# Half of the input ahead of the first weights, the SSM's swaps of halves in SyncE's queue, and the last LayerNorm pass in halves on VectorE

## The chip, the cores and the metric

The kernel runs on one core of one Trainium2 chip. The metric is the time of one execution in device microseconds, the median of three runs. The profile is that of one further execution, recorded by the hardware profiler.

## What is computed

Two decoder layers over x of 256 tokens by 1024 channels, all in float32. In each layer a mixer and a feed-forward part stand one behind the other, and each is modulated by shift, scale and gate columns that are computed from the conditioning vector c. Inside the mixer a state-space model (SSM, a diagonal complex scan) and a sparse attention run side by side on one input projection. Cut to what matters:

```python
cond_in = jax.nn.silu(c)
for l in range(DEPTH):
    mod = cond_in @ w_cond[l] + b_cond[l]              # 6 x 1024 columns
    sh1, sc1, gt1, sh2, sc2, gt2 = split(mod, 6)
    u = x * (1.0 + sc1) + sh1
    z = u @ w_in[l]                                    # u_ssm, q, k, v, index q/k/w, two gates
    y_ssm = s5_branch(u_ssm, ...)                      # scan over time, GELU, GLU
    y_attn = dsa_branch(q, k, v, q_idx, k_idx, w_idx)  # top-64 keys of each query, attention
    h = (sigmoid(g_ssm) * (y_ssm @ p_ssm) + sigmoid(g_attn) * (y_attn @ p_attn)) @ w_out[l]
    x = layer_norm(ALPHA * x + (1 + gt1) * h, ln1_g[l], ln1_b[l])
    u = x * (1.0 + sc2) + sh2
    f = (silu(a) * b) @ w_down[l]                      # a, b = split(u @ w_gate_up[l])
    x = layer_norm(ALPHA * x + (1 + gt2) * f, ln2_g[l], ln2_b[l])
return x
```

## The kernel before, in words

The tokens are held as two tiles of 128 rows: `X[:, 0]` and `X[:, 1]`, each 128 x 1024. Every product with a weight is done in three passes with a high and a low part of both operands (`hi`, `lo`, `aTh`, `aTl`). A weight block of 512 KB is loaded into a `raw` tile by a DMA that SyncE issues (L351), ScalarE casts it to `hi` (L388), VectorE subtracts to get `lo` (L389), and TensorE multiplies (L1396, L1476). The blocks stand in one list; a pump (`st.pump_dma`) issues the next loads of that list, as many as there are free tiles, so what stands first in the program stands first in SyncE's queue. SyncE works its queue in order, and a load whose tile is not free yet holds up those behind it.

**The start.** c is loaded, then the conditioning's weights (`w_cond`, 512 KB a block) and the first blocks of `w_in`. TensorE transposes X in 16 pieces (L1527: four of the first half, then twelve that need the second half too), transposes constants of the SSM (L546, L567), and makes the first columns of the modulation from four `w_cond` blocks, which the program calls group 0 here (L448, 32 matmuls); then come the first products of the input projection (L1547), and group 1 of the modulation from the next four blocks (L448 again). The first half of x is loaded in ScalarE's queue (L1566), the second in SyncE's (L1568).

**The SSM's scan** (`ssm_run`). For each of two halves h = 0, 1 there is a set of tiles 128 x 512, which the traces call `s` (h = 0) and `k` (h = 1). Per half VectorE multiplies by cosine and sine (L863, L864), adds (L865) and scans along time (L866). Then `swap_halves` copies the scan's result with partitions 0 to 63 and 64 to 127 exchanged into another tile of the set, by two DMAs of 128 KB (L508, L509). Later VectorE multiplies the scan's result by the cosine (`s2`, L872), the swapped tile by the sine (`s3`, L873), and subtracts (`s4`, L878); TensorE reads what `s4` wrote (L886). `swap_halves` is also called twice while the SSM of layer 1 is prepared, around 330 us. Where `s2`, `s3` and `s4` stand in VectorE's order among the other work (the `lo` subtractions, the indexer's scores `sco` L1044, the rounds of top-k L1049 and L1050) is decided by the program's own order of steps when it is built.

**The end.** `ln_out(t)` is the last LayerNorm for each of the two token tiles: mean and variance (L1247, L1248), a power -0.5 on GpSimd (L1249), then columns 0 to 831 in two passes on VectorE and columns 832 to 1023 by ScalarE and GpSimd, with one store each from SyncE.

Of the kernel before, what the change touches and what calls it, by code (L numbers as in the profile page):

```python
# [10 lines left out]
AF = mybir.ActivationFunctionType  # L11
ALU = mybir.AluOpType
# [3 lines left out]
D = 1024  # L16
# [156 lines left out]
def kernel(  # L173
# [11 lines left out]
    V, A, P, PE, SP = nc.vector, nc.scalar, nc.gpsimd, nc.tensor, nc.sync  # L185
    NRAW, NHL, AHEAD = 6, 4, 2
    LO_P = (1, 2)
    OUT_A = 832
    GLU_AT = "ga0"
    DENSE = ((None, 2, 2, 2, 2, 2, 2, 2, 2, 2, 2), (2, 4, 4, 4, 4, 2), (2, 4, 4, 4, 4, 4, 4, None, None, None, None),  # L190
             (None,) * 6)
# [19 lines left out]
    def sbt(shape, tag, dt=F32, bufs=1):  # L211
        return sb.tile(shape, dt, tag=tag, bufs=bufs, name=nm(tag))
# [79 lines left out]
    def start(gen):  # L292
        t = Task(gen)
        tasks.append(t)
        return t
# [100 lines left out]
    st = Stream()  # L396
# [108 lines left out]

    def swap_halves(o, i):

        P.dma_start(o[0:64], i[64:128])  # L508
        P.dma_start(o[64:128], i[0:64])  # L509


    ssm = [dict() for _ in range(depth)]
# [1 line left out]
    def ssm_prep(l, w0, w, we):  # L514
# [72 lines left out]
        if l == 0:  # L587
            V.tensor_scalar(X1, pc, sg1, None, ALU.mult)
            A.copy(X2, turned_c(1))
        else:  # L590
            A.copy(cc, pc)
            V.tensor_scalar(X1, cc, sg1, None, ALU.mult)
            swap_halves(X2, cc)
# [22 lines left out]
        if l:  # L616
            swap_halves(pb2, pb1)
# [177 lines left out]
    def ssm_run(l, acc, tab):  # L795
# [59 lines left out]
        for h in range(2):  # L855
            S_, a_, r_, g_ = [w4s[h][:, i] for i in range(4)]
            cs, sn, rh = phase[h]

            p, q = tp_t(), tp_t()
            for m in range(4):  # L860
                PE.transpose(p[:, 128 * m:128 * m + 128], S_[:, 128 * m:128 * m + 128], ident)
                PE.transpose(q[:, 128 * m:128 * m + 128], g_[:, 128 * m:128 * m + 128], ident)
            V.tensor_tensor(a_, cs, p, ALU.mult)  # L863
            V.tensor_tensor(r_, sn, q, ALU.mult)  # L864
            place("s1", V).tensor_tensor(a_, a_, r_, ALU.add)  # L865
            V.tensor_tensor_scan(r_, rh, a_, 0.0, ALU.mult, ALU.add)  # L866
            swap_halves(S_, r_)
            yield
# [292 lines left out]
    X = sbt([128, NT, D], "X")  # L1161
# [62 lines left out]
    def rows_of(vec, tag):  # L1224
        r = sbt([128, D], tag)
        SP.dma_start(r, vec.unsqueeze(0).broadcast_to((128, D)) if len(vec.shape) == 1 else vec.broadcast_to((128, D)))
        return r
# [16 lines left out]
    def ln_scale(t, stats):  # L1244

        mv = sbt([128, 4], "mv", bufs=2)
        V.bn_aggr(mv[:, 0:2], stats[:, t])  # L1247
        V.tensor_scalar(mv[:, 2:3], mv[:, 1:2], EPS, None, ALU.add)  # L1248
        root[0] = P.tensor_tensor(mv[:, 1:2], mv[:, 2:3], mhalf, ALU.pow)  # L1249
        return mv  # L1250
# [7 lines left out]

    def ln_out(t, stats, gbc, bbc):
        mv = ln_scale(t, stats)  # L1260
        a, b = slice(0, OUT_A), slice(OUT_A, D)
        V.scalar_tensor_tensor(X[:, t, a], X[:, t, a], mv[:, 0:1], gbc[:, a], ALU.subtract, ALU.mult)
        V.tensor_scalar(mv[:, 3:4], mv[:, 0:1], mv[:, 1:2], -1.0, ALU.mult, ALU.mult)
        V.scalar_tensor_tensor(X[:, t, a], X[:, t, a], mv[:, 1:2], bbc[:, a], ALU.mult, ALU.add)
        SP.dma_start(out[0, 128 * t:128 * t + 128, a], X[:, t, a])
        A.activation(X[:, t, b], X[:, t, b], AF.Identity, scale=mv[:, 1:2], bias=mv[:, 3:4])
        P.tensor_tensor(X[:, t, b], X[:, t, b], gbc[:, b], ALU.mult)
        P.tensor_tensor(X[:, t, b], X[:, t, b], bbc[:, b], ALU.add)
        SP.dma_start(out[0, 128 * t:128 * t + 128, b], X[:, t, b])
        return []  # L1270


# [289 lines left out]
    A.dma_start(K1, consts[:, 0:K_1])  # L1562
    b0 = start(first_bias())
    b0.step()
    st.pump_dma(1)
    A.dma_start(X[:, 0], x[0, 0:128])  # L1566
    st.pump_dma(2)
    SP.dma_start(X[:, 1], x[0, 128:256])  # L1568
    prep = start(ssm_prep(0, *W_PREP[0]))
    st.pump_dma(4)  # L1570
    prep.step()
# [26 lines left out]
    for l in range(depth):  # L1598
# [90 lines left out]
        gbc = rows_of(ln1_g[l], "c1")  # L1689
        bbc = rows_of(ln1_b[l], "c2")  # L1690
# [87 lines left out]
        gbc = rows_of(ln2_g[l], "c1")  # L1778
        bbc = rows_of(ln2_b[l], "c2")
# [4 lines left out]
        def ffn_norm(t, acc, last=l + 1 == depth, gtb=gtb, stats=stats, gbc=gbc, bbc=bbc):  # L1784
            n = 256 if last else 512
            ln_part(acc, t, D - n, n, gtb, stats)
            return ln_out(t, stats, gbc, bbc) if last else ln_end(t, stats)
# [40 lines left out]
```

## Time and profile before

| what | value |
|---|---|
| median of three runs | 942.22 us (940.75 to 945.61) |
| the profiled execution, its time | 946.86 us |
| its span in the trace | 945.1 us |
| TensorE busy | 882.7 us (93%) |
| VectorE busy | 679.6 us (72%) |
| ScalarE busy | 407.5 us (43%) |
| GpSimd busy | 72.0 us (8%) |
| mean granted TensorE clock | 0.978 |
| moved by DMA | 201.37 MB, mean 213 GB/s |

The span is the time from the first to the last instruction of the program; the 1.8 us around it belong to the launch. TensorE works nearly all the time, so a change pays where TensorE waits, or at the two ends of the program where it has no work.

### The profile page before, as it was taken

What the parts mean: (1) busy time and instruction counts of PE and PEld (TensorE: products, weight loads), DVE (VectorE), ACT (ScalarE), POOL (GpSimd) and SP (SyncE); (2) the same over time, 40 slices, a digit from 0 to 9 for tenths busy, and PEclk for the clock granted to TensorE, in tenths of its full rate; (3) what the DMA queues carried; (4) which work ended last, traced back from release to release, by engine and by line L of the source; (5) the groups of instructions that cost most, each with busy time, mean ns of one, the idle gap of its engine ahead of it and who ended that gap; (6) DMA issues with size and microseconds to landing.
All of it is one profiled execution on the core that took longest, in us unless ns stands there. A gap on an engine that the chain in (4) does not pass through costs nothing.

```text
span 945.1 us, 16044 instructions
## 1 busy us (share of the span) xinstructions
PE 882.7 (93%) x6295; PEld 745.6 (79%) x6295; DVE 679.6 (72%) x1189; ACT 407.5 (43%) x599; POOL 72.0 (8%) x145
## 2 busy tenths in 40 slices
PE   4899899999998999999998977999999999999993
PEld 3557677887976799998886955799988799999893
DVE  2798899855677588766667987995658776556463
ACT  2134325735345444444344522566445544444430
POOL 4001610000000000000000360000000000000002
PEclk9999899999999999999999988999999999999997
DMA  9965986876776677778665796566737285556521
GB/s 291 309 223 129 239 270 221 278 236 211 280 253 203 208 250 265 241 251 287 212 223 175 204 220 231 187 213 203 223 112 247 107 268 180 182 185 192 175 94 45
DMA packets 104856, 201.37 MB, mean 213 GB/s; under 512 B 9688, under 2 KB 33220, under 8 KB 104780
## 3 DMA queue, kind: packets, MB, share of 16 engines
q1 hardware_dynamic: 99612, 190.76, 62.4%
q0 software_dynamic: 3584, 8.11, 4.0%
q10 hardware_dynamic: 1584, 1.48, 0.6%
q8 instruction: 49, 0.80, 0.4%
q14 instruction: 27, 0.22, 0.1%
HBM read 195.65 MB, written 2.05 MB: 209 GB/s over the span
## 4 chain that ended last, share of the span: by engine, by line
PE 60%; DVE 16%; DMA 12%; issue 5%; ACT 4%; POOL 1%; SPq 0%; POOLq 0%; ACTq 0%; DVEq 0%
PE acc L1476 33%; PE acc L1396 15%; DMA raw<-in_w_in_dram 6%; DVE lo L389 3%; PE cnd L476 3%; PE acc L1547 2%; ACT hi L388 1%; DMA X<-in_x_dram 1%; DMA raw<-in_w_out_dram 1%; PE bk L1138 1%; DMA raw<-in_w_gate_up_dram 1%; DMA c<-gt 1%; DVE stats L1240 1%; DMA s<-rope 1%; PE bk L1105 1%
## 5 line engine op out<-in xcount | busy, mean ns | idle before, releaser
L389 DVE TENSOR_TENSOR lo<-raw,hi 128x1024 fp32r<-128x1024 f32 (+2 forms) x217 | 262.1, 1213 | 156.9 <-ACT hi L388 156.1
L388 ACT CAST hi<-raw 128x1024 fp32r<-128x1024 f32 (+2 forms) x217 | 225.0, 1042 | 321.1 <-PE acc L1476 113.7
L1476 PE MATMUL acc<-aTh,hi 128*128 128x256 f32 x832 | 137.4, 287 | 0.0
L1476 PE MATMUL acc<-aTh,lo 128*128 128x256 f32 x832 | 132.3, 281 | 0.0
L1476 PE MATMUL acc<-aTl,hi 128*128 128x256 f32 x832 | 132.3, 281 | 0.0
L1476 PEld LDWEIGHTS acc<-aTh,hi 128*128 128x128 f32 x832 | 113.2, 188 | 17.6 <-issue 13.1
L1476 PEld LDWEIGHTS acc<-aTl,hi 128*128 128x128 f32 x832 | 113.1, 188 | 0.0
L1476 PEld LDWEIGHTS acc<-aTh,lo 128*128 128x128 f32 x832 | 113.0, 188 | 0.0
L1396 PE MATMUL acc<-hi,aTh 128*128 128x512 f32 (+2 forms) x200 | 64.2, 406 | 5.5 <-DVE tmp L966 3.8
L1396 PE MATMUL acc<-lo,aTh 128*128 128x512 f32 (+2 forms) x200 | 61.3, 392 | 0.7 <-DVE lo L389 0.7
L1396 PE MATMUL acc<-hi,aTl 128*128 128x512 f32 (+2 forms) x200 | 61.1, 391 | 0.3 <-DVE aTl L1672 0.3
L1249 POOL TENSOR_TENSOR mv<-mv,mhalf 128x1 f32<-128x1 f32 x8 | 6.9, 857 | 614.2 <-DVE mv L1248 372.4
L1396 PEld LDWEIGHTS acc<-hi,aTh 128*128 128x128 f32 x200 | 34.8, 194 | 18.8 <-issue 7.6
L1396 PEld LDWEIGHTS acc<-lo,aTh 128*128 128x128 f32 x200 | 37.4, 194 | 9.4 <-DVE lo L389 1.6
L1396 PEld LDWEIGHTS acc<-hi,aTl 128*128 128x128 f32 x200 | 37.5, 194 | 9.3 <-DVE aTl L1672 1.1
L476 PE MATMUL cnd<-raw,csil 128*32 128x512 f32 x320 | 42.6, 605 | 0.0
L1396 PE MATMUL acc<-hi,MT 128*128 128x512 f32 (+1 forms) x144 | 36.9, 353 | 0.0
L1396 PE MATMUL acc<-lo,MT 128*128 128x512 f32 (+1 forms) x144 | 36.3, 349 | 0.0
L1396 PE MATMUL acc<-hi,q 128*128 128x512 f32 (+1 forms) x144 | 36.3, 349 | 0.0
L835 POOL DMA_DIRECT2D MT<-KT_d x64 | 33.6, 532 | 20.8 <-DMA MT<-KT_d 13.5
L1396 PEld LDWEIGHTS acc<-lo,MT 128*128 128x128 f32 x144 | 24.0, 188 | 4.0
L1396 PEld LDWEIGHTS acc<-hi,q 128*128 128x128 f32 x144 | 24.1, 188 | 3.8
(401 smaller groups left out, 1450.7 us busy)
## 6 DMA issues: line engine op xcount, KB each, us to landing
raw<-in_w_cond_dram SPq DMA_DIRECT2D x96, 512.0 KB, 4.8
raw<-in_w_gate_up_dram SPq DMA_DIRECT2D x88, 512.0 KB, 4.9
raw<-in_w_in_dram SPq DMA_DIRECT2D x62, 512.0 KB, 5.3
raw<-in_w_down_dram SPq DMA_DIRECT2D x43, 512.0 KB, 4.4
raw<-in_p_attn_dram SPq DMA_DIRECT2D x16, 512.0 KB, 3.7
raw<-in_w_out_dram SPq DMA_DIRECT2D x16, 512.0 KB, 6.5
MT<-KT_d POOLq DMA_DIRECT2D x64, 64.0 KB, 5.7
raw<-in_p_ssm_dram SPq DMA_DIRECT2D x16, 256.0 KB, 5.4
```

What stands on the lines that cost most here:

```text
L388: i = A.copy(hv, ch.rv)
L389: j = place("lo", ch.lo_on).tensor_tensor(lv, ch.rv, hv.bitcast(F32), ALU.subtract)
L476: PE.matmul(acc[32 * g:32 * g + 32, 0:w], csil[:, kt], rv[:, w * (g % per):w * (g % per) + w], start=kt == 0, stop=kt == KD - 1, tile_posi ...
L835: P.dma_start(MT[16 * s:16 * s + 16, :, k], bass.AP(tensor=KT_d.tensor, offset=KT_d.offset + k * 16 * 1920 + 16 * s, ap=[[1920, 16], [240, ...
L1105: PE.matmul(p[:, nk * (h - h0):nk * (h - h0) + nk], X["qT"][:, 4 * kv + h, 128 * t:128 * t + 128], X["kT"][:, kv, 0:nk], start=True, stop= ...
L1138: PE.matmul(p, X["V"][:, s, 128 * kv:128 * kv + 128], PT[:, s].rearrange("p h q -> p (h q)"), start=s == 0, stop=s == t)
L1240: V.bn_stats(stats[:, t, 6 * (c // 256):6 * (c // 256) + 6], X[:, t, c:c + 256])
L1249: root[0] = P.tensor_tensor(mv[:, 1:2], mv[:, 2:3], mhalf, ALU.pow)
L1396: PE.matmul(o, st_of(kt, t)[part == 2], (ch.lv if part == 1 else ch.hv)[:, k, :], start=kt == blk.first and part == 0, stop=kt == blk.last ...
L1476: PE.matmul(acc[:, 256 * i:256 * i + 256], w[:, k, n:n + 128], mov(kt)[part == 2], start=kt == blk.first and part == 0 and i == 0, stop=kt ...
L1547: PE.matmul(ac[t][:, 0:blk.n], AT32[:, t, kt], ch.rv[:, k], start=kt == 0 and (i < 2 or t == 0), stop=kt == KD - 1, skip_group_check=i == 2)
```

## The change

Three places in the code change, and with them the order in which the program puts VectorE's and SyncE's steps.

1. The load of `X[:, 1]` is issued ahead of the conditioning's weights, and the pump call that put one weight block in front is gone.
2. `swap_halves` issues its two DMAs from SyncE instead of GpSimd, for all six calls.
3. `ln_out` works on all 1024 columns with VectorE: one first pass of 1024 columns, and the second pass in two halves of 512, of which the first is stored from SyncE and the second from ScalarE. `OUT_A` goes.

```diff
--- before.py
+++ after.py
@@ -185,7 +185,6 @@
     V, A, P, PE, SP = nc.vector, nc.scalar, nc.gpsimd, nc.tensor, nc.sync
     NRAW, NHL, AHEAD = 6, 4, 2
     LO_P = (1, 2)
-    OUT_A = 832
     GLU_AT = "ga0"
     DENSE = ((None, 2, 2, 2, 2, 2, 2, 2, 2, 2, 2), (2, 4, 4, 4, 4, 2), (2, 4, 4, 4, 4, 4, 4, None, None, None, None),
              (None,) * 6)
@@ -505,8 +504,8 @@
 
     def swap_halves(o, i):
 
-        P.dma_start(o[0:64], i[64:128])
-        P.dma_start(o[64:128], i[0:64])
+        SP.dma_start(o[0:64], i[64:128])
+        SP.dma_start(o[64:128], i[0:64])
 
 
     ssm = [dict() for _ in range(depth)]
@@ -1258,15 +1257,11 @@
 
     def ln_out(t, stats, gbc, bbc):
         mv = ln_scale(t, stats)
-        a, b = slice(0, OUT_A), slice(OUT_A, D)
-        V.scalar_tensor_tensor(X[:, t, a], X[:, t, a], mv[:, 0:1], gbc[:, a], ALU.subtract, ALU.mult)
-        V.tensor_scalar(mv[:, 3:4], mv[:, 0:1], mv[:, 1:2], -1.0, ALU.mult, ALU.mult)
-        V.scalar_tensor_tensor(X[:, t, a], X[:, t, a], mv[:, 1:2], bbc[:, a], ALU.mult, ALU.add)
-        SP.dma_start(out[0, 128 * t:128 * t + 128, a], X[:, t, a])
-        A.activation(X[:, t, b], X[:, t, b], AF.Identity, scale=mv[:, 1:2], bias=mv[:, 3:4])
-        P.tensor_tensor(X[:, t, b], X[:, t, b], gbc[:, b], ALU.mult)
-        P.tensor_tensor(X[:, t, b], X[:, t, b], bbc[:, b], ALU.add)
-        SP.dma_start(out[0, 128 * t:128 * t + 128, b], X[:, t, b])
+        V.scalar_tensor_tensor(X[:, t], X[:, t], mv[:, 0:1], gbc, ALU.subtract, ALU.mult)
+        for h, q in enumerate((SP, A)):
+            s = slice(512 * h, 512 * h + 512)
+            V.scalar_tensor_tensor(X[:, t, s], X[:, t, s], mv[:, 1:2], bbc[:, s], ALU.mult, ALU.add)
+            q.dma_start(out[0, 128 * t:128 * t + 128, s], X[:, t, s])
         return []
 
 
@@ -1562,10 +1557,9 @@
     A.dma_start(K1, consts[:, 0:K_1])
     b0 = start(first_bias())
     b0.step()
-    st.pump_dma(1)
     A.dma_start(X[:, 0], x[0, 0:128])
+    SP.dma_start(X[:, 1], x[0, 128:256])
     st.pump_dma(2)
-    SP.dma_start(X[:, 1], x[0, 128:256])
     prep = start(ssm_prep(0, *W_PREP[0]))
     st.pump_dma(4)
     prep.step()
```

SyncE's queue at the start of the program, before (the first nine loads; `raw` from `w_cond` are group 0's four blocks, `hi` and `lo` tiles here also receive raw blocks of `w_in`):

```order
L1561 DMA c8_13_86<-in_c_dram 8x128
L432 DMA b16_14_89<-in_b_cond_dram 16x128
L351 DMA raw_15_91<-in_w_cond_dram 128x4x256
L351 DMA raw_16_94<-in_w_cond_dram 128x4x256
L1568 DMA X_7_80<-in_x_dram 128x1024
L351 DMA raw_17_97<-in_w_cond_dram 128x4x256
L351 DMA raw_18_99<-in_w_cond_dram 128x4x256
L351 DMA hi_23_117<-in_w_in_dram 128x2x512
L351 DMA lo_24_119<-in_w_in_dram 128x2x328
```

and after the change:

```order
L1556 DMA c8_13_86<-in_c_dram 8x128
L431 DMA b16_14_89<-in_b_cond_dram 16x128
L1561 DMA X_7_80<-in_x_dram 128x1024
L350 DMA raw_15_93<-in_w_cond_dram 128x4x256
L350 DMA raw_16_95<-in_w_cond_dram 128x4x256
L350 DMA raw_17_97<-in_w_cond_dram 128x4x256
L350 DMA raw_18_99<-in_w_cond_dram 128x4x256
L350 DMA hi_23_117<-in_w_in_dram 128x2x512
L350 DMA lo_24_119<-in_w_in_dram 128x2x328
```

The 512 KB of `X` (128 x 1024) stand ahead of all weights now, and were third among them.

SyncE's queue in layer 1, where the scans are (about 542 to 570 us of the trace of before); `raw` are weight blocks, `c2` and `c1` the LayerNorm's bias and gain, `c0` a gate row. Before:

```order
L351 DMA raw_873_5646<-in_w_in_dram 128x2x512
L351 DMA raw_874_5648<-in_w_in_dram 128x2x512
L351 DMA raw_875_5650<-in_w_in_dram 128x2x512
L1226 DMA c2_1104_7292<-in_ln1_b_dram 128x1024
L351 DMA raw_876_5652<-in_w_in_dram 128x2x512
L351 DMA raw_884_5700<-in_w_cond_dram 128x1024
L1226 DMA c0_1102_7288<-gt10_76 128x1024
L351 DMA raw_885_5702<-in_w_cond_dram 128x1024
L351 DMA raw_886_5704<-in_w_in_dram 128x2x512
L351 DMA raw_887_5706<-in_w_in_dram 128x2x512
```

and after the change:

```order
L350 DMA raw_873_5646<-in_w_in_dram 128x2x512
L350 DMA raw_874_5648<-in_w_in_dram 128x2x512
L507 DMA s8_852_5513<-s8_852_5513 64x512
L508 DMA s8_852_5513<-s8_852_5513 64x512
L350 DMA raw_875_5650<-in_w_in_dram 128x2x512
L350 DMA raw_876_5652<-in_w_in_dram 128x2x512
L350 DMA raw_884_5700<-in_w_cond_dram 128x1024
L507 DMA k8_853_5514<-k8_853_5514 64x512
L508 DMA k8_853_5514<-k8_853_5514 64x512
L350 DMA raw_885_5702<-in_w_cond_dram 128x1024
L1225 DMA c0_1102_7288<-gt10_76 128x1024
L1225 DMA c2_1104_7292<-in_ln1_b_dram 128x1024
```

The two copies of `s8` and the two of `k8` are the swaps, 128 KB each. They came in from GpSimd's queue, and each pair stands between weight loads now. Behind these rows `c1` (the LayerNorm's gain) has its place before `raw_887_5706`; before the change it stood behind `raw_914_5930`.

VectorE's order in layer 1, before, from `lo_908_5915` on, which is the subtraction that the trace shows at 576.16 us (`s8` is half 0, `k8` half 1; L873 is `s3`, L878 `s4`):

```order
L389 TENSOR_TENSOR lo_908_5915<-raw_886_5704,hi_907_5914 128x1024
L1044 SCALAR_TENSOR_TENSOR sco0_900_5759<-sp_899_5758,widx_831_5393,sco0_900_5759 128x128 x5
L389 TENSOR_TENSOR lo_910_5919<-raw_887_5706,hi_909_5918 128x1024
L1044 SCALAR_TENSOR_TENSOR sco0_900_5759<-sp_899_5758,widx_831_5393,sco0_900_5759 128x128
L873 TENSOR_TENSOR s8_852_5513<-c1_800_5140,s8_852_5513 128x512
L1044 SCALAR_TENSOR_TENSOR sco0_900_5759<-sp_899_5758,widx_831_5393,sco0_900_5759 128x128
L878 TENSOR_TENSOR s8_852_5513<-s8_852_5513 128x16x31
L1044 SCALAR_TENSOR_TENSOR sco0_900_5759<-sp_899_5758,widx_831_5393,sco0_900_5759 128x128
L1049 MAX m8_904_5833<-sco0_900_5759 128x8
L873 TENSOR_TENSOR k8_853_5514<-c1_800_5140,k8_853_5514 128x512
```

and after the change, from the product L862 (L863 before) of half 1 on, which the trace of before shows at 556.55 us:

```order
L862 TENSOR_TENSOR k8_853_5514<-c0_799_5139,bk_861_5589 128x512
L872 TENSOR_TENSOR s8_852_5513<-c1_800_5140,s8_852_5513 128x512
L863 TENSOR_TENSOR k8_853_5514<-c1_800_5140,bk_862_5590 128x512
L964 TENSOR_TENSOR rope_866_5622<-acc_827_5374,K_2_69 128x256
L965 TENSOR_TENSOR tmp_867_5623<-acc_827_5374,K_2_69 128x256
L877 TENSOR_TENSOR s8_852_5513<-s8_852_5513 128x16x31
L864 TENSOR_TENSOR k8_853_5514<-k8_853_5514 128x512
L968 TENSOR_TENSOR rope_866_5622<-rope_866_5622,tmp_867_5623 128x256
L865 SCALAR_TENSOR_TENSOR k8_853_5514<-c2_801_5141,k8_853_5514 128x512
L388 TENSOR_TENSOR lo_881_5691<-raw_874_5648,hi_880_5690 128x1024
L871 TENSOR_TENSOR k8_853_5514<-c0_799_5139,k8_853_5514 128x512
L388 TENSOR_TENSOR lo_889_5709<-raw_875_5650,hi_888_5708 128x1024
```

`s3` and `s4` of half 0 moved from behind `lo_908_5915` and `lo_910_5919` to the stretch between the products of half 1, some 20 us earlier by the trace of before. `s3` and `s4` of half 1 follow the same way: `s3` directly behind the last row here, `s4` four rows after it, ahead of `lo_897_5747`. The second half's last GELU product (L900 before, L899 after) stood ahead of `lo_938_6066` and stands behind it now. TensorE's order does not change.

## Rows read from the trace of the kernel before

**Rows 1.** The page: busy time by engine.

```profile
PE 882.7 (93%) x6295; PEld 745.6 (79%) x6295; DVE 679.6 (72%) x1189; ACT 407.5 (43%) x599; POOL 72.0 (8%) x145
```

**Rows 2.** What TensorE waited for: us in total, times, longest.

```profile
PE bk L1527 <- DMA X<-in_x_dram: 9.4, 2, 8.8
PE bk L886 <- DVE s L878: 6.5, 1, 6.5
```

**Rows 3.** TensorE's timeline at the start: start us, us, work [idle before, releaser].

```profile
15.01 2.79 PE L1527 MATMUL bk<-K,X 128*128 128x128 f32 x12 [8.85 <-DMA X<-in_x_dram]
...
21.71 3.64 PE L448 MATMUL bk<-raw,csil 128*32 128x256 f32 x32
...
35.77 1.93 PE L448 MATMUL bk<-raw,csil 128*32 128x256 f32 x32
```

**Rows 4.** SyncE's queue (number 1): packets, MB, share, from 0 to 10, 18, 33 us.

```profile
q1 hardware_dynamic: 1025, 1.00, 33.8%
...
q1 hardware_dynamic: 2524, 3.08, 57.0%
...
q1 hardware_dynamic: 7237, 8.47, 80.2%
```

**Rows 5.** TensorE in layer 1, timeline.

```profile
575.12 0.63 PE L1396 MATMUL acc<-hi,aTl 128*128 128x512 f32 x2
582.27 0.66 PE L886 MATMUL bk<-E,s 128*32 128x128 f32 x8 [6.52 <-DVE s L878]
...
586.82 0.66 PE L1069 MATMUL bk<-K,rope 128*128 128x128 f32 x4
...
605.68 1.03 PE L910 MATMUL bk<-K,p 128*128 128x128 f32 x8
```

**Rows 6.** VectorE in layer 1, timeline.

```profile
552.84 1.22 DVE L866 TENSOR_TENSOR_SCAN s<-c,s 128x512 f32<-128x512 f32 x1
...
557.15 0.68 DVE L864 TENSOR_TENSOR k<-c,bk 128x512 f32<-128x512 f32 x1
...
576.16 1.23 DVE L389 TENSOR_TENSOR lo<-raw,hi 128x1024 fp32r<-128x1024 f32 x1 [4.12 <-ACT hi L388]
...
580.59 0.69 DVE L873 TENSOR_TENSOR s<-c,s 128x512 f32<-128x512 f32 x1
...
599.30 1.20 DVE L900 TENSOR_TENSOR p<-k 128x512 f32<-128x512 f32 x1
```

**Rows 7.** Windows in layer 1: busy (count) of PE, PEld, DVE, ACT, POOL; clock, DMA, GB/s.

```profile
582.00:584.00 2.00, 1.73 (x14) 0.77 (x14) 1.97 (x7) 0.00 (x0) 0.00 (x0) 0.50 0.55 209
...
588.00:600.00 12.00, 12.00 (x113) 8.30 (x112) 11.90 (x24) 6.57 (x10) 0.00 (x0) 1.00 0.45 139
```

**Rows 8.** GpSimd in layer 1, timeline.

```profile
560.63 0.57 POOL L508 DMA_DIRECT2D s<-s  x1
```

**Rows 9.** The swaps' second DMA, line L509, all six calls.

```profile
DMA to landing us min/median/max: 3.4/5.7/8.3
```

**Rows 10.** TensorE in layer 0, timeline.

```profile
145.05 0.43 PE L886 MATMUL bk<-E,s 128*32 128x128 f32 x8
...
148.16 0.65 PE L1082 MATMUL bk<-K,rope 128*128 128x128 f32 x4
```

**Rows 11.** The end: VectorE, GpSimd and SyncE, timeline.

```profile
931.92 1.07 DVE L1262 SCALAR_TENSOR_TENSOR X<-X,mv,c 128x832 f32<-128x832 f32 x1
932.08 1.32 POOL L1249 TENSOR_TENSOR mv<-mv,mhalf 128x1 f32<-128x1 f32 x1 [2.66 <-DVE mv L1248]
...
935.17 0.59 POOL L1268 TENSOR_TENSOR X<-X,c 128x192 f32<-128x192 f32 x1
935.78 0.33 SPq L1269 DMA_DIRECT2D out_dram<-X  x1
```

**Rows 12.** The program's closing line L1823: durations ns least/median/most, starts of first and last.

```profile
L1823 POOLq DRAIN  x3: 46/102/9126, 935.1 to 944.8; - x3
L1823 SPq DRAIN  x3: 7/7/7, 938.0 to 944.5; - x3
```

## Prediction

> **What bounds the kernel now.** I read the page first: TensorE is busy 882.7 of 945.1 us [rows 1], so all that can be won is the 62 us in which it has nothing to do. Then TensorE's waits. The two that this change can touch are the longest: 9.4 us for X at the start, and one of 6.5 us in layer 1 for VectorE's `s4` [rows 2]. Then the timeline at those two places and at the end, for what stands behind each wait.
>
> At the start, 12 transposes of X begin at 15.01 after 8.85 us of idling, the SSM's transposes follow, and the 32 matmuls of group 0 run from 21.71 to 25.35 [rows 3]. SyncE's queue had moved 1.00 MB by 10 us, 3.08 by 18 and 8.47 by 33 [rows 4]: 0.36 MB/us from 18 to 33. The second half of X was its third block of 0.52 MB, so it ended at 1.58 MB.
>
> In layer 1 TensorE stops at 575.75 and goes on at 582.27 when `s4` of half 0 is there [rows 5]. VectorE was not short of time before: it stood idle 4.12 us until 576.16, in front of a `lo` whose weights came late, and `s3` and `s4` stood behind that `lo` and began at 580.59 [rows 6]. The scan of half 0 had ended at 554.06 [rows 6], but the swap was issued only at 560.63 [rows 8], in a GpSimd queue filled with other loads. So the wait is one of order. Behind it the granted clock stands at 0.50, the lower of the two levels (1.2 GHz), after 6.5 us without matmuls [rows 7]; half 0 took 4.55 us from 582.27 to 586.82 [rows 5], where the same work in layer 0 took 3.11 [rows 10]. Wait and slow clock cost 6.5 + 1.4 = 8.0 us.
>
> At the end, GpSimd's last operation ends at 935.76 and SyncE's last store is issued at 935.78 [rows 11]; GpSimd's closing drain begins at 935.1 and takes 9.13 us, to 944.3, and the span ends 0.8 us later [rows 12].
>
> **The start.** X is now the first large block of SyncE's queue, 0.54 MB in instead of 1.58. The queue passes 0.54 MB before 10 us, where it has 1.00 [rows 4]: X lands between 6 and 9 instead of 14.9, and TensorE's transposes start some 6 to 8 us earlier. No byte is saved; the bytes of group 0's weights come no sooner. Their four blocks end at 2.63 MB, which [rows 4] put at 10 + 1.63 / 2.08 x 8 = 16.3 us. So group 0 can end at about 17.5 to 18.5 instead of 25.35. But group 1's last block stands at 8.34 MB of the queue (X 0.52, eight blocks of `w_cond` 4.19, eight loads of `w_in` 3.63, each by its size), that is at 32.6 us by [rows 4], and the issue of those loads was already limited by the bytes. Before, group 1 began at 35.77 and ended at 37.70 [rows 3]. Now it can end at 32.6 plus up to 2.7 us of landing and processing, 33.3 to 35.3: the gain falls to 2.4 to 4.4 us. I take -3, with -6 if the bytes come faster than that and -1 if an emptier TensorE runs at the lower clock or the SSM's preparation on VectorE stays the chain.
>
> **The swaps.** Twelve DMAs of 128 KB go from GpSimd to SyncE. In layer 0 (around 129 to 134 us) TensorE came to half 0 at 145.05 without waiting [rows 10], so there is nothing to win; each pair only puts a wait for a scan in front of SyncE's next weight loads. The cover is the weight blocks already in the tiles, since TensorE's longest waits name no weights [rows 2]; I take 0, with bounds 0 and +3, and rival (c) below if the cover is gone. The same cover serves the two calls near 330 us: 0.
>
> In layer 1 SyncE can issue the swap of half 0 at once when the scan ends, 554.1. The swaps landed 3.4 to 8.3 us after their issue, median 5.7 [rows 9]; by the median 559.8. VectorE meets `s3` of half 0 at 557.15, the place of the product that stood there [rows 6], and would stand still 0.3 to 5.2 us; I take 2, since it no longer shares GpSimd's crowded queue. A stall like it follows for half 1, whose scan ended at 560.57 before and whose swap stands behind three weight blocks. Queued behind the stalls on VectorE are the products of half 1 and two `lo`; the 4.12 us of idling before 576.16 cover both [rows 6]. Then `s4` of half 0 is there by some 562, TensorE goes on at 575.75 at full clock, and is 8.0 us earlier from 586.82 on.
>
> What is late next? VectorE. From 576.16 to 600.50, the end of half 1's last GELU product, it did 24.3 us of work [rows 6] with hardly a gap: 11.90 of 12.00 us from 588 [rows 7]. Out of this stretch go the four steps `s3` and `s4`, 4 x 0.69 = 2.8; into it, ahead of that product, comes one `lo`, 1.23 [rows 6]. So it ends at 24.3 - 2.8 + 1.2 = 22.8 after 576.16, at 598.9. TensorE's L910 needs it; it came at 605.68 [rows 5] and would come 8.0 earlier, at 597.7. It waits 1.2 there, and 6.8 are left. As VectorE is now the bound through this stretch, any stall not covered comes straight off. I take -4.5, two thirds of it, with bounds 0 and -8.
>
> The Trainium skill, "DMA: Bandwidth & Descriptors", section "Queues, rings and completion order", has a rule that speaks against this edit: each DMA engine takes turns between the queue rows with work, packet by packet, while one row's ring is drained in order. By it a swap in GpSimd's row took turns with SyncE's weights, and in SyncE's row it stands behind every weight block already issued. No row here shows a swap in SyncE's queue; at the start the trace agrees as to order, since X came third and landed third. For half 1 the rule gives up to 1.05 MB ahead of it, which is a rival below.
>
> **The end.** For the second token tile, VectorE's first pass over 1024 columns takes 1.07 x 1024/832 = 1.32 us, from 931.92 to 933.24, under the power that ends at 933.40 [rows 11]. Two passes of 512 at 0.69 each (the row of `s3`, same width [rows 6]) end at 934.8, and ScalarE's store is issued then, 1.0 us ahead of 935.78. GpSimd's last operation is now the power: 2.36 us earlier than 935.76. If the end follows GpSimd's drain by its fixed 8.5 us, that is -2.4; if it follows the last store, -1.0; if neither, 0. In the trace GpSimd's drain is the longest by far and SyncE was through at 938.0 [rows 12], so I take -2. For the first tile the extra work of VectorE lies under TensorE's last matmuls: 0.
>
> **Sum.** -3 - 4.5 - 2 = -9.5 us. The profiled execution took 946.86, 4.6 above the median of the three runs, 942.22; its terms are differences, so I take them off the median: 933 us.
>
> **The rivals.**
> (a) *The gain in layer 1 is eaten.* VectorE's stalls are not covered, or its `lo` become the bound, so that TensorE merely waits elsewhere; the start gives 1 to 3 and the end 0 to 1. For it: 11.90 of 12 us busy [rows 7]. Against: the four steps leave that stretch. -1 to -4.5: 938 to 941.
> (b) *All 8 us come through,* with up to 6 at the start and 2 at the end: -12 to -16, 926 to 930. For it: TensorE's only long wait goes [rows 2]. Against: the 1.2 us at L910 worked out above.
> (c) *Slower: the swaps queue behind weights.* A swap in SyncE's order waits for its scan with weights behind it, and for the bytes of weights ahead of it. Up to 1.05 MB (two blocks) at 209 GB/s (0.21 MB/us), as in one window there [rows 7], is 5 us on top of the best landing of 3.4 [rows 9]. In layer 0, where `s3` of half 1 now stands ahead of a `lo`, and in layer 1 alike, VectorE then stands still for 5 us or more. Up to the idle 4.1 us this costs nothing; beyond it each us delays a `lo`, and TensorE, once empty for 6 us, pays for the lower clock as well, 8.0 us as above. One such wait in layer 0 with layer 1 given away and the start's 3 us kept: +5 or more, 947 to 950. Against: GpSimd's landings were no shorter than 3.4 either, and TensorE had not waited for weights in these stretches [rows 2].
> (d) *Nothing happens:* X's early landing is swallowed by group 1 and the end is fixed: within 1 us of 942.
>
> **How the numbers follow.** Forecast (-6 to -12, 930 to 936) 0.47; (b) 0.15; (a) 0.21; (d) 0.06; (c) 0.11. What a measurement of this kernel can tell from no change is about 0.5%, 4.7 us. Faster by more takes the forecast and (b): 0.62. Within it lie (a) and (d), 0.27. Slower: 0.11. The range from 926 to 941 leaves out (c), half of (d) and a little at the lower end, under 2 in 10.
>
> **What would show it.** Right: TensorE's wait for X falls under 4 us, group 1 ends 2 to 4 us earlier; the wait of 6.5 for `s4` is gone and L886 of half 0 takes about 3.1 us; VectorE shows a new wait for the swap's DMA of some 2 us, and L910 a small one for L900's product; GpSimd's drain begins after the power. Wrong: a wait of TensorE for `lo` or of VectorE for the swap above 4 us, in layer 0 above all; group 1 still at 35.8; or a span that ends the same time after the last store as before.

## The result, and the profile after

The changed kernel took 934.2 us (median of five runs, 932.2 to 936.5) against 944.3 for the kernel before: a ratio of 0.9896, 95% interval 0.9869 to 0.9923. A second set of runs gave 0.9931 (0.9904 to 0.9959). The forecast was 933. The profiled execution has a span of 930.4 us. Two single executions, one of the kernel "group 1 early" (1430 us) and one of the version "both, layer 1's swaps only" (1078 us), ran at a mean granted clock of 0.56 and 0.76, and the medians and ratios below leave them out.

The page's line of busy time, beside [rows 1]:

```profile
PE 878.5 (94%) x6295; PEld 739.9 (80%) x6295; DVE 679.9 (73%) x1189; ACT 406.0 (44%) x597; POOL 63.2 (7%) x129
```

TensorE's waits, as in [rows 2] (us in total, times, longest):

```profile
PE bk L447 <- DMA raw<-in_w_cond_dram: 4.8, 4, 3.8
...
PE bk L909 <- DVE p L899: 2.6, 2, 1.7
...
PE bk L909 <- ACT sp L1038: 1.4, 1, 1.4
PE bk L1522 <- DMA X<-in_x_dram: 1.3, 2, 0.8
```

The two long waits are gone: X costs 1.3 instead of 9.4, and the 6.5 for `s4` is not in the list. In their place stand 4.8 us for the modulation's weights and some 4 for the GELU product (`p`) and for ScalarE's `sp`, an input of the indexer's scores.

TensorE at the start, as in [rows 3]:

```profile
6.87 2.79 PE L1522 MATMUL bk<-K,X 128*128 128x128 f32 x12 [0.77 <-DMA X<-in_x_dram]
...
13.85 1.94 PE L447 MATMUL bk<-raw,csil 128*32 128x256 f32 x16
...
28.11 1.07 PE L447 MATMUL bk<-raw,csil 128*32 128x256 f32 x16
33.01 1.08 PE L447 MATMUL bk<-raw,csil 128*32 128x256 f32 x8 [3.83 <-DMA raw<-in_w_cond_dram]
...
35.53 3.45 PE L1542 MATMUL acc<-hi,MT 128*128 128x512 f32 x4
```

The same stretch in windows (busy of the five engines, then clock, DMA share, GB/s):

```profile
28.00:33.00 5.00, 1.18 (x17) 0.42 (x16) 3.26 (x5) 0.00 (x0) 0.00 (x0) 0.87 1.10 351
33.00:36.00 3.00, 2.56 (x17) 0.87 (x18) 0.00 (x0) 0.27 (x1) 0.00 (x0) 0.50 1.10 348
36.00:39.00 3.00, 3.00 (x6) 0.80 (x5) 0.69 (x1) 0.83 (x2) 0.00 (x0) 0.58 1.10 349
39.00:42.00 3.00, 2.80 (x14) 1.98 (x14) 2.72 (x7) 0.17 (x1) 0.00 (x0) 1.00 1.10 354
```

The transposes come 8.1 us earlier and group 0 ends about 7 earlier. Group 1 ends only 2.1 earlier (35.60 instead of 37.70), since its last two blocks are not there; the DMA engines are busy throughout at 350 GB/s. The four matmuls behind group 1 begin 3.0 us earlier. After the empty 3.8 us the clock stands at 0.50, the lower level, and these four take 3.45 us. In the trace of before they took 1.98:

```profile
38.49 1.98 PE L1547 MATMUL acc<-hi,MT 128*128 128x512 f32 x4 [0.79 <-DVE MT L1519]
```

Behind them 1.5 us of the lead are left, and 1.0 at 68 us.

VectorE in layer 1, beside [rows 6]:

```profile
555.87 0.69 DVE L872 TENSOR_TENSOR s<-c,s 128x512 f32<-128x512 f32 x1 [2.77 <-DMA s<-s]
...
565.16 0.69 DVE L872 TENSOR_TENSOR k<-c,k 128x512 f32<-128x512 f32 x1 [1.84 <-DMA k<-k]
```

SyncE's queue there, which issued the swaps (the second copy of each pair, and for half 1 also the weight block ahead of it and the first copy):

```profile
550.56 0.93 SPq L508 DMA_DIRECT2D s<-s  x1
...
555.89 0.41 SPq L350 DMA_DIRECT2D raw<-in_w_cond_dram  x1
560.54 0.47 SPq L507 DMA_DIRECT2D k<-k  x1
561.05 0.59 SPq L508 DMA_DIRECT2D k<-k  x1
```

And TensorE, beside [rows 5]:

```profile
571.04 0.42 PE L885 MATMUL bk<-E,s 128*32 128x128 f32 x8
...
573.81 0.66 PE L1068 MATMUL bk<-K,rope 128*128 128x128 f32 x4
...
593.75 0.63 PE L909 MATMUL bk<-K,p 128*128 128x128 f32 x4 [0.92 <-DVE p L899]
595.78 0.66 PE L909 MATMUL bk<-K,p 128*128 128x128 f32 x4 [1.41 <-ACT sp L1038]
```

VectorE stalls 2.77 and 1.84 us for the swaps and goes on 5.3 and 4.1 us after their issue. TensorE starts half 0 without a wait and finishes it in 2.8 us instead of 4.55; 0.9 and 1.4 us are given back at L909.

The end, beside [rows 11], GpSimd's last operation:

```profile
920.61 1.46 POOL L1248 TENSOR_TENSOR mv<-mv,mhalf 128x1 f32<-128x1 f32 x1 [4.90 <-DVE mv L1247]
```

And the closing line, as in [rows 12]:

```profile
L1817 POOLq DRAIN  x3: 46/102/9002, 920.6 to 930.1; - x3
L1817 SPq DRAIN  x3: 7/7/7, 925.8 to 929.9; - x3
```

The drain (a DRAIN instruction in GpSimd's queue at the close of the program) begins with the power and takes 9.0 us, where it took 9.1 before, so it ends earlier.

### The profile page after: what moved, and what is told of

It is laid out like the page before. It is cut to its first block, busy times and chain, and to the rows that moved or that the text cites. A ratio compares the mean times of both kernels' runs of the same rounds, so it can differ in the third digit from the quotient of the medians.

```text
span 930.4 us, 16050 instructions
## 1 busy us (share of the span) xinstructions
PE 878.5 (94%) x6295; PEld 739.9 (80%) x6295; DVE 679.9 (73%) x1189; ACT 406.0 (44%) x597; POOL 63.2 (7%) x129
## 4 chain that ended last, share of the span: by engine, by line
PE 58%; DVE 18%; DMA 14%; issue 5%; ACT 3%; SPq 0%; POOL 0%; POOLq 0%; DVEq 0%; ACTq 0%
PE acc L1471 34%; PE acc L1391 13%; DMA raw<-in_w_in_dram 5%; DVE lo L388 4%; PE cnd L475 3%; DMA raw<-in_w_cond_dram 2%; PE acc L1542 2%; ACT hi L387 1%; DMA raw<-in_w_down_dram 1%; DMA raw<-in_w_out_dram 1%; PE bk L1137 1%; PE bk L1104 1%; DMA raw<-in_w_gate_up_dram 1%; DVE sco L1043 1%; DVE tmp L965 1%
## 5 line engine op out<-in xcount | busy, mean ns | idle before, releaser
L1391 PEld LDWEIGHTS acc<-hi,MT 128*128 128x128 f32 x144 | 23.8, 188 | 4.3 <-issue 0.8
```

The costliest lines, as they stand in the source:

```text
L1391: PE.matmul(o, st_of(kt, t)[part == 2], (ch.lv if part == 1 else ch.hv)[:, k, :], start=kt == blk.first and part == 0, stop=kt == blk.last ...
```

## The experiments

TensorE's order is the same in all these kernels, so the start of one and the same matmul can be set beside that of the kernel before. The table gives the difference, in us (negative is earlier), at marks named by the time that they have in the trace of before, for one profiled execution each. The last two columns are worked out: what is won from 519 to 623 us (layer 1's scans), and from the mark at 911 to the end of the span. The profiled execution of before was 2 us above the median of its runs, and single executions differ by some us, mostly between 194 and 519 us, where even kernels without an edit there win 1 to 3 us; times are therefore read from the medians, and places from the table.

| kernel | 38 | 68 | 112 | 173 | 519 | 587 | 623 | 911 | end | layer 1 | last stretch |
|---|---|---|---|---|---|---|---|---|---|---|---|
| changed | -3.0 | -1.0 | -0.8 | +1.2 | -3.8 | -13.0 | -10.3 | -11.5 | -14.7 | -6.5 | -3.2 |
| changed, again | -3.0 | -1.8 | -2.1 | +1.8 | -1.2 | -8.7 | -4.2 | -4.9 | -8.0 | -3.0 | -3.2 |
| X alone | -3.0 | +2.7 | +3.3 | +2.9 | +0.8 | +0.9 | +0.9 | +0.3 | +0.2 | +0.1 | 0.0 |
| swaps alone | -0.2 | +0.9 | +0.9 | +4.3 | +3.2 | -4.8 | -2.0 | -2.6 | -3.6 | -5.2 | -1.0 |
| end alone | -0.8 | -0.4 | -0.6 | +0.4 | -2.0 | -2.3 | -2.3 | -2.7 | -4.4 | -0.3 | -1.7 |
| layer 1's swaps only | -2.8 | +0.8 | +0.6 | +2.4 | +1.2 | -8.6 | -3.9 | -4.6 | -7.0 | -5.2 | -2.5 |
| group 1 early | -6.4 | -5.7 | -6.8 | -4.0 | -9.8 | -18.9 | -12.7 | -12.9 | -16.1 | -2.9 | -3.2 |
| root off GpSimd | -2.5 | -0.6 | -0.7 | +1.0 | -1.4 | -11.1 | -6.4 | -6.9 | -14.1 | -5.1 | -7.2 |
| both, layer 1's swaps only | -6.8 | -5.5 | -5.5 | -5.9 | -8.5 | -17.1 | -12.7 | -13.8 | -21.0 | -4.2 | -7.2 |
| that, again (base) | -8.3 | -5.9 | -6.1 | -5.7 | -8.5 | -17.1 | -12.9 | -13.3 | -20.5 | -4.4 | -7.2 |
| base, layer 0 on SyncE | -8.1 | -5.4 | -5.3 | -5.3 | -7.3 | -16.5 | -10.6 | -10.9 | -17.8 | -3.3 | -7.0 |
| base, no swap on SyncE | -6.6 | -5.8 | -5.8 | -5.0 | -7.4 | -7.4 | -7.4 | -8.0 | -15.0 | 0.0 | -7.0 |
| base, X late | -0.1 | +1.6 | +2.2 | +1.8 | -0.3 | -8.2 | -6.5 | -7.5 | -14.7 | -6.2 | -7.2 |

**One edit at a time.** X alone (the kernel of before, with only this):

```diff
-    st.pump_dma(1)
     A.dma_start(X[:, 0], x[0, 0:128])
+    SP.dma_start(X[:, 1], x[0, 128:256])
     st.pump_dma(2)
-    SP.dma_start(X[:, 1], x[0, 128:256])
```

> The kernel of before with the first edit alone: X[:, 1] ahead of the conditioning's weights. My theory (the term of -3 in the prediction): TensorE's wait for X shrinks from 8.9 us to about 0.8, group 1 of the modulation ends 2 to 4 us earlier, and what is won there stays to the end: -3 us. Rival, from the trace of the changed kernel: the gain is 3.0 us behind group 1 and falls to 1.0 by 60 us, because TensorE waits 3.8 us for the weights of group 1 and the matmuls behind the wait run slower; then the whole is worth -1 us, 0 to -1.5. Both expect a wait of 3 to 5 us for the w_cond block of group 1. Nothing changes around 145, 580 and 930 us.

Measured: 943.8 against 945.0 us, ratio 0.9985 (0.9961 to 1.0010). TensorE's wait for group 1's weights, and windows of its trace:

```profile
33.02 0.64 PE L448 MATMUL bk<-raw,csil 128*32 128x256 f32 x8 [2.76 <-DMA raw<-in_w_cond_dram]
```

```profile
36.00:39.00 3.00, 3.00 (x4) 0.71 (x3) 0.69 (x1) 0.84 (x2) 0.00 (x0) 0.50 1.10 348
39.00:42.00 3.00, 3.00 (x10) 2.31 (x10) 2.28 (x6) 0.17 (x1) 0.00 (x0) 0.50 1.10 354
42.00:46.00 4.00, 4.00 (x10) 2.34 (x10) 3.43 (x6) 0.00 (x0) 0.00 (x0) 0.74 0.55 174
```

The lead of 3.0 at 38 us is there, and the slow clock lasts into the 42 to 46 window: at 68 us this execution is 2.7 behind. The rival holds: the edit alone is worth little or nothing. The wait is shorter here than in the changed kernel (2.76 instead of 3.83 us), because TensorE came to it later (it began group 1 at 29.19 instead of 28.11): it had been at the lower clock from 14 to 27 us already, where the changed kernel, with much the same work, was not. The same window, X alone first, then the changed kernel:

```profile
14.00:27.00 13.00, 10.83 (x52) 5.31 (x45) 8.05 (x42) 2.32 (x6) 0.00 (x0) 0.50 1.08 360
14.00:27.00 13.00, 10.91 (x56) 5.13 (x53) 8.08 (x41) 2.34 (x6) 0.00 (x0) 1.00 1.08 360
```

So the length of the slow stretch behind the wait is not a thing of the edit alone; it differs between executions.

Swaps alone:

```diff
-        P.dma_start(o[0:64], i[64:128])
-        P.dma_start(o[64:128], i[0:64])
+        SP.dma_start(o[0:64], i[64:128])
+        SP.dma_start(o[64:128], i[0:64])
```

> The second edit alone: all swaps issued from SyncE, with the order of VectorE that follows from it. Theory: layer 1 wins about 8 us at the matmuls of half 0 (no wait of 6.5, no slow clock) and gives 2 to 3 back at L910; layer 0 loses about 2 at L910, where TensorE waits for the last GELU product; together -4 to -6 us. Rival: layer 0's loss in the trace of the changed kernel came with the other edits or the execution, and the swaps are worth -5 to -8. Told apart by TensorE's wait at L910 of layer 0 (before: 0.5 us; theory: 1.5 or more here; rival: 0.5).

Measured: 938.6, ratio 0.9943 (0.9920 to 0.9965), 5.4 us (3.3 to 7.6). Layer 1 gives 5.2 net. Layer 0 loses 3.4 between 112 and 173, but not at L910 as expected, where no wait is listed: TensorE waits 3.0 us at L1082 for ScalarE's copy of the scan's product. That copy stood behind a cast, and the cast behind a weight block that came late:

```profile
154.00 1.04 ACT L388 CAST hi<-raw 128x1024 fp32r<-128x1024 f32 x1 [4.36 <-DMA raw<-in_w_in_dram]
```

So the time agrees with the theory, and the place in layer 0 does not.

The end alone (the edit of `ln_out`, as in the diff of the change):

> The third edit alone: the last pass on VectorE in halves, stores from SyncE and ScalarE. Theory (the prediction's -2, by the trace of the changed kernel 3): the end follows GpSimd's closing drain, which lasts 9 us from where GpSimd's last operation begins; that is now the power, so the stretch from TensorE's last matmul to the end shrinks by 3 us: -3. Rival: the end follows the last store; then -1. Both expect no difference before 905 us.

Measured: 946.2, ratio 1.0000 (0.9978 to 1.0022). The trace shows 1.7 us won in the last stretch; the interval allows up to 2.1. By time alone this edit is not told from nothing. GpSimd's drain took 9.99 us in this execution and 9.13 in that of before, which took 0.9 off the gain; with the swaps alone it took 8.15, and there the last stretch is 1.0 shorter without any edit at the end. So about 1 us of that column is the drain's own variation.

**Layer 1's swaps only** (the changed kernel, the others back on GpSimd):

```diff
-    def swap_halves(o, i):
+    def swap_halves(o, i, q=P):
-        SP.dma_start(o[0:64], i[64:128])
-        SP.dma_start(o[64:128], i[0:64])
+        q.dma_start(o[0:64], i[64:128])
+        q.dma_start(o[64:128], i[0:64])
...
-            swap_halves(S_, r_)
+            swap_halves(S_, r_, SP if l else P)
```

> The changed kernel, but the swaps of layer 0's scan and of the preparation of layer 1 go back to GpSimd; only those of layer 1's scan stay on SyncE. If the swaps on SyncE cost layer 0 two us (TensorE's wait at its L909 of 1.7 instead of 0.5, VectorE's p late), this one is about 2 us faster than the changed kernel: -12 against before. If the loss in layer 0 was of the execution or of another edit, it is the same as the changed kernel within 1 us: -10.

Measured: 936.1, ratio 0.9908 (0.9876 to 0.9941), 8.7 us (5.6 to 11.7): less than either expectation by its middle, and too wide to choose between them, since the changed kernel itself gave 9.8 and 6.5 in its two sets. Its start fell into the long slow clock as X alone did.

**The changed kernel again, and the causes at both ends.**

> The changed kernel once more, beside the three below. By its first five runs -9.8 us against before. By the sum of the single edits' medians (X -1.4, swaps -5.4, end 0) it would be -7; by the terms read in its trace (start -1, layer 0 +2, layer 1 -5.2, end -3) also -7. If this run gives -9 or more, something beyond the three terms is in it, or the single runs read low.

Measured: 938.8, ratio 0.9931 (0.9904 to 0.9959), 6.5 us (3.9 to 9.1). It agrees with the sum of the single edits, about 7; the -9.8 of the first set lies just outside this interval, and the two sets' intervals overlap between 7.3 and 9.1.

Group 1's weights together:

```diff
-                st.q.append(Chunk("raw", w_rows(w_cond[0], 512 * r, 4, c0, 256), (4, 256)))
+                st.q.append(Chunk("raw", w_rows(w_cond[0], 512 * r, 4, c0, 256), (4, 256), False, i == 1 and j == 1))
```

> The changed kernel, with the last two weight blocks of group 1 loaded into two of the tiles that w_in's third blocks had, so that group 1's four blocks stand together in SyncE's queue, 1.38 MB further ahead; w_in's third blocks come later and are needed only behind group 2. Theory: X's early landing was swallowed because TensorE then waits 3.8 us for group 1's bytes and comes out of the wait at the lower clock; 1.38 MB at 0.355 MB/us is 3.9 us, so the wait goes, the clock stays at 1.00 between 28 and 40 us, and group 1 ends near 31 instead of 35.5: 4 to 5 us faster than the changed kernel at 68 us and, if kept, at the end. Rival: the start is bound elsewhere (VectorE's affine columns, or the bytes of group 2), and at 68 us at most 1 us is left.

Measured: 930.8, ratio 0.9882 (0.9846 to 0.9918). That is 4.6 us under the changed kernel beside it by the two ratios and 8.0 by the two medians; the two intervals overlap slightly. Windows of its trace:

```profile
28.00:33.00 5.00, 3.99 (x40) 2.07 (x39) 4.28 (x7) 1.21 (x2) 0.00 (x0) 1.00 1.08 365
33.00:36.00 3.00, 3.00 (x14) 1.85 (x13) 2.03 (x6) 0.17 (x1) 0.00 (x0) 1.00 1.10 349
```

And TensorE's timeline, the last of group 1 and the first products behind it:

```profile
30.43 0.61 PE L447 MATMUL bk<-hi,csil 128*32 128x256 f32 x8
32.06 1.98 PE L1542 MATMUL acc<-hi,MT 128*128 128x512 f32 x4 [1.01 <-DVE MT L1514]
```

No wait of TensorE for weights of more than 0.6 us, clock 1.00, 1.98 instead of 3.45 for the four matmuls, 5.7 us ahead at 68 us. The theory holds.

The root off GpSimd:

```diff
-        mv = ln_scale(t, stats)
+        mv = sbt([128, 4], "mv", bufs=2)
+        V.bn_aggr(mv[:, 0:2], stats[:, t])
+        V.tensor_scalar(mv[:, 2:3], mv[:, 1:2], EPS, None, ALU.add)
+        A.activation(mv[:, 3:4], mv[:, 2:3], AF.Sqrt)
+        V.reciprocal(mv[:, 1:2], mv[:, 3:4])
```

> The changed kernel, with the inverse root of the last LayerNorm by a square root on ScalarE and a reciprocal on VectorE instead of the power on GpSimd, so that GpSimd's last operation lies near 733 us. Theory: the end is GpSimd's closing drain, 8 to 10 us from the start of its last operation; without that operation the end follows the last store's landing, and the stretch from TensorE's last matmul to the end falls from 11.7 to about 8 us: -3 to -4 against the changed kernel. Rival: the drain lasts until 9 to 10 us behind the last work of any engine, or follows the stores; then the end gains only what the shorter chain gives, 0 to -1.

Measured: 932.9, ratio 0.9885 (0.9862 to 0.9909), under the changed kernel beside it by 4.3 us by the ratios and 5.9 by the medians; these intervals overlap slightly too. Its end in the timeline:

```profile
925.16 0.20 ACT L1262 ACTIVATE mv<-mv 128x1 f32<-128x1 f32 x1 [6.15 <-DVE mv L1261]
926.24 0.16 DVE L1263 RECIPROCAL mv<-mv 128x1 f32<-128x1 f32 x1
...
927.88 0.35 ACTq L1268 DMA_DIRECT2D out_dram<-X  x1
```

And its closing line:

```profile
L1821 POOLq DRAIN  x3: 46/102/8112, 737.6 to 930.7; - x3
L1821 SPq DRAIN  x3: 7/7/7, 930.1 to 930.4; - x3
```

GpSimd's first drain has moved to 737.6, behind its last operation of the middle of the program, and the end comes 3.1 us after the last store's issue at 927.88. In the changed kernel it came 6.8 us after the same store's issue, with a span of 930.4:

```profile
923.55 0.35 ACTq L1264 DMA_DIRECT2D out_dram<-X  x1
```

The last stretch is 7.2 us shorter than before, 4.0 of it against the changed kernel; the chain up to the store's issue became only 0.3 shorter. The theory holds: GpSimd's drain closed all eight executions in which GpSimd worked at the end.

Both, and only layer 1's swaps on SyncE:

> Both together, and the swaps of layer 0 and of the preparation back on GpSimd (only layer 1's scan swaps on SyncE). Theory: -4 from the start, -3 to -4 from the end, -1 to -2 from layer 0 against the changed kernel: -17 to -20 against before. Rival: as in the two above, then no more than -3 against the changed kernel.

Measured: 926.2, ratio 0.9842 (0.9802 to 0.9881), which is 14.9 us (11.2 to 18.7) under the kernel before; 17 to 20 were expected, which the interval reaches in part. This version beats both kernels. The layer 0 part of the expectation is not seen, as a run below shows.

**One thing taken back from that base.**

> The best version so far (group 1's weights together, the root off GpSimd, only layer 1's scan swaps on SyncE) once more, as the base of the three below: -17 us against before, as in its first runs.

Measured: 927.8, ratio 0.9825 (0.9797 to 0.9853), 16.5 us where 17 were expected.

Layer 0's scan swaps on SyncE too (`swap_halves(S_, r_, SP)`):

> The base, with the swaps of layer 0's scan on SyncE too. If they cost layer 0 about 2 us, as the traces between 112 and 173 us say (2.1, 3.8, 3.4, 2.8 and 1.7 lost in five executions with them, -0.4 to 1.7 in four without), this is 2 us slower than the base, and its trace loses 2 to 3 us more between those marks. Rival: what those traces show is chance; the same as the base.

Measured: 927.1, ratio 0.9819 (0.9783 to 0.9854): the same as the base, and its trace loses nothing between 112 and 173 us. The theory that the swaps as such cost layer 0 two us falls: five executions with all swaps on SyncE lost 1.7 to 3.9 there, this one 0.0. The order of the steps does not make the difference. Up to the preparation of layer 1, around 330 us, all engines and SyncE's queue have the same order here as in the kernel with group 1 early, which was 6.8 us ahead at 112 us (5.3 here) and lost 2.8. What differs is when SyncE comes to the first swap. Its queue in layer 0, with group 1 early, then here:

```profile
122.07 0.34 SPq L350 DMA_DIRECT2D raw<-in_w_cond_dram  x1
124.46 0.55 SPq L507 DMA_DIRECT2D s<-s  x1
...
121.61 0.34 SPq L350 DMA_DIRECT2D raw<-in_w_cond_dram  x1
122.17 0.55 SPq L507 DMA_DIRECT2D s<-s  x1
```

With group 1 early SyncE stands 2.0 us between the weight block and the swap, until the scan of half 0 ends at 124.43, and its next weight loads stand behind; here it stands 0.2 us. In the other four executions that lost, it stood 2.0 us as well. So the loss goes with the wait that the prediction put in front of SyncE's weight loads. No run changes that wait alone, so it is not shown to be the cause, and why this execution escaped it stays open.

No swap on SyncE (`swap_halves(S_, r_, P)`):

> The base, with all swaps on GpSimd. If the swap's move is worth 4 to 5 us in layer 1, this is 4 to 5 us slower than the base, and its trace has the wait of 6 to 7 us of TensorE at the matmuls of half 0 in layer 1 and the lower clock behind it. Rival: with the earlier start the loads of GpSimd's queue lie elsewhere and the wait is mostly gone; less than 2 us slower.

Measured: 932.9, ratio 0.9873 (0.9849 to 0.9897), 5.1 us slower than the base by the medians, 4.5 by the ratios. TensorE's longest wait:

```profile
PE bk L885 <- DVE s L877: 7.1, 1, 7.1
```

The wait is back, and the theory holds.

X late (the first edit undone in the base):

> The base, with X[:, 1] back behind the first two weight blocks, the first edit undone. The edit alone was worth -1.4 with 3.7 us of waiting for group 1's weights behind it; where these come early, it should be worth what it brings the first transposes, less what VectorE's preparation of the SSM needs: this is 4 to 6 us slower than the base. Rival: the early place of X is worth nothing even here, because the bytes of group 1 set the start: within 1 us of the base.

Measured: 931.8, ratio 0.9872 (0.9837 to 0.9907), 4.0 us slower than the base by the medians (4.4 by the ratios), at the lower edge of what was expected. TensorE's wait for X is back:

```profile
PE bk L1526 <- DMA X<-in_x_dram: 9.9, 2, 9.1
```

So X's early place is worth about 4 us where group 1's weights follow, and 1.4 (between 3.7 won and 0.9 lost) where they don't.

## Why the prediction was right, and where its terms were off

The total was right (-9.5 forecast; -9.8 and -6.5 in two sets, both inside the range of 926 to 941). Its terms:

- **The start, -3: too large, measured about 0 to -1.** The step to group 1 was nearly right: the transposes began at 6.87, group 1 was bound by its bytes, and it ended 2.1 us earlier, where 2.4 to 4.4 were worked out; the matmuls behind it were 3.0 us ahead. The step that failed is that the rest of the start would keep this lead. The text named the lower clock as a bound of the range (-1) and did not price it: waiting for group 1 empties TensorE for 3.6 to 5.1 us in all, and the matmuls behind run at 0.50 for some 5 to 10 us. In the five executions with X early and group 1 late the lead shrank by 1.2 to 5.7 us between the marks at 38 and 68, and was then between 1.8 ahead and 2.7 behind. That group 1 early brings -5.7 there shows the cause; it takes away the wait and the slow clock together, so the two are not told apart.
- **Layer 1, -4.5: right in size, and in its first half as worked out.** Ten executions with these swaps on SyncE won 2.9 to 6.5 from 519 to 623 us, 4.6 in the mean, and three without were within 0.3 of nothing. The gain up to the mark at 587 was 7.5 to 9.8, 8.8 in the mean, where 8.0 was worked out: VectorE stalled 2.77 and 1.84 us in the changed kernel, about as much as the 4.12 us of idling that were to cover it, and half 0 ran at full clock. What was too small is what is given back behind it: 1.2 in the working, and 1.7 to 6.2, 4.2 in the mean, by the table. The changed kernel's waits at L909 were 0.92 us for VectorE's `p` and 1.41 for ScalarE's `sp`, which was not in the working. In seven of the ten executions the lower clock followed as well. The three at 1.00 gave back 1.7 to 2.8, the seven 4.2 to 6.2. The third that the text took off its 6.8 us, for stalls that are not covered, happened to pay for this: the number is right, in part by luck.
- **The end, -2: somewhat small by the traces.** The last stretch became 1.7 to 3.2 us shorter with the edit, 2.8 in the mean of five, of which about 1 us can be the drain's own variation; the time of this edit alone shows 0 with an uncertainty of 2.1. The end follows GpSimd's drain, the first of the two ways named, and the root off GpSimd shows that it is the drain and not the last store.
- **Layer 0, 0: undecided.** Five executions lost 2.8 us in the mean between 112 and 173, two of them more than the bound of +3, for waits of TensorE on ScalarE's copy and on VectorE's product; in all five SyncE's swap waited 2.0 us for the scan in front of weight loads. One with the swaps on SyncE did not wait and did not lose.
- **Rival (c)**, the swap held up behind weight blocks, did not come in layer 1: the swap of half 1 was there 4.1 us after its issue. The ring's order that the Trainium skill, "DMA: Bandwidth & Descriptors", section "Queues, rings and completion order", states shows no cost there: by the trace SyncE's last weight block before it was issued at 555.89, 4.7 us ahead of the swap's first copy, and VectorE's stall was shorter than for half 0.

Most was given back in layer 1 with group 1 early. A window of that kernel behind L909, and one of the changed kernel around the same work, whose clock stayed up:

```profile
590.00:596.00 6.00, 5.37 (x17) 4.49 (x18) 5.82 (x10) 4.59 (x6) 0.00 (x0) 0.50 0.41 123
589.00:603.00 14.00, 11.67 (x72) 8.29 (x71) 13.75 (x27) 7.35 (x10) 0.00 (x0) 1.00 0.50 156
```

The terms as measured sum to between about -5 and -8, and the single edits to about -7. The first set's -9.8 is thus nearer to the forecast than the terms are, and that nearness is luck: the start was read too high by 2 to 3 us.

## What to carry to other kernels

A load that is moved forward pays only as far as the next load in the same queue is not already the bound: count the bytes to the second consumer, too, and bring that one's bytes forward with it. If an engine is sped up into an empty stretch, price the lower clock behind the stretch. At the end of a program look at which engine's closing drain ends last (in these kernels GpSimd's), and see whether that engine's last operation can go elsewhere.

## What the runs showed of the hardware that was not expected

GpSimd's closing drain took 8.1 to 10.0 us, from the start of GpSimd's last operation, in the eight executions where it worked at the end, and cost nothing where its last operation lay some 190 us earlier. And the lower clock behind an empty stretch had no fixed length. In the changed kernel TensorE was empty for 3.8 us up to 33.0 and the clock was back at 1.00 in the window from 39 us; in X alone it was empty for 2.8 us up to the same point and the clock was still at 0.50 in the window from 39 to 42. X alone had also stood at 0.50 from 14 to 27 us, and so had the kernel with layer 1's swaps only, the other one with the long slow stretch. At the mark at 68 the start of the changed kernel was 1.0 us ahead and X alone 2.7 behind.
